# Four opening products taken in turns, norm factors folded into the operand operations, and two weight sums reordered in a two-layer encoder kernel

## The chip, the cores and the metric

The kernel runs on one core of one Trainium2 chip. The core has a matrix engine (TensorE, PE in the profile, with its weight loads as PEld), VectorE (DVE), ScalarE (ACT), GpSimd (POOL) and SyncE (SP). SP, ACT and POOL issue DMAs; a DMA that adds to its destination is issued from POOL here. The metric is the device time of one execution in microseconds, as the median of several runs; lower is better.

## What is computed

An encoder of two layers over 512 tokens and 16 learned ones (528 columns), width 1024. A layer is a feed-forward half step, a mixer of two parallel branches, and a second feed-forward half step; a norm closes the whole.

```python
def rmsnorm(x, g):
    return x * lax.rsqrt(jnp.mean(x * x, axis=-1, keepdims=True) + EPS) * g

def swiglu(x, w_gate, w_up, w_down):
    return (jax.nn.silu(x @ w_gate) * (x @ w_up)) @ w_down

for l in range(DEPTH):                                     # DEPTH = 2
    h = h + 0.5 * swiglu(rmsnorm(h, norm_gains[l, 0]), ffn_w_gate[l, 0], ...)
    h = h + mixer(rmsnorm(h, norm_gains[l, 1]), ...)       # GLA branch + attention branch, gated
    h = h + 0.5 * swiglu(rmsnorm(h, norm_gains[l, 2]), ffn_w_gate[l, 1], ...)
return rmsnorm(h, final_norm)[:, N_META:]
```

The hidden width of the feed-forward part, D_FF, is 2816. All data are float32.

## The kernel before

The hidden state stands in SBUF as eight chunks of 128 channels by 528 tokens. Every float32 product is made of three matmuls on rounded parts: each operand is split into `hi`, a copy rounded to the matrix engine's format, and `lo`, the rest; hi·hi, hi·lo and lo·hi are summed. The split of a weight of 128 x 1024 is one cast on ScalarE (`whi`, line 226) and one subtraction on VectorE (`wlo`, line 227). There are four buffers for `whi` and four for `wlo`, so the fifth weight's cast waits until the first weight's matmuls are done.

**The gate and up products.** The 2816 hidden columns are 11 pairs of 256. For each pair the product with x is a 2 x 2 block product (two hidden blocks, two token halves, the channels as even and odd chunks) carried out with seven block products instead of eight. `product_of_pair` makes one of them: four operand pairs (k = 0 to 3, chunks 2k and 2k+1), gate and up, three matmuls each, 24 matmuls of 128 x 264. Products 1, 2 and 4 use a weight block straight from memory (w11, w12, w22). The other four use weight sums: product 7 uses s3 = w21 - w11, product 6 uses s2 = w22 + s3, product 5 uses s1 = w21 + w22, product 3 uses s4 = s2 - w12.

`Weights.sums` makes these sums. ScalarE writes the negative of w11 or w12 (line 177); POOL then adds blocks with accumulating DMAs (line 182): s3 += w21, s2 += s3, s1 = w21 += w22, s4 += s2, one after the other in POOL's own order, each 512 KB. s2 and s1 are first loaded by SP into two short-lived buffers (`wsb`); the next pair's loads into these wait until the split of the old one, and for s2 also the add into s4, is done. `s3` and `s4` stand in three longer-lived buffers (`wsa`).

**The operands.** `Norm.pair` (line 432) makes one operand pair from two chunks: it scales both by the norm's gain (line 436), forms the four sums and differences `t12` and `t34` (lines 451 to 455), and splits seven blocks of 264 columns into `hi` and `lo` tiles `xc` (lines 443, 444, 448, 449). The factor of the root mean square (`rs`) comes later: eight squares (line 426) on ScalarE, seven adds (line 430) on VectorE, then the mean by a matmul with constants (line 398), a logarithm, an exponential and a Newton step.

**The order.** `ffn_steps` writes the order of the products out by hand. At the start of each of the four feed-forward parts, here called an opening, it is products 1 and 2 of pair 0, products 1 and 2 of pair 1, then products 6, 5, 7, 4 and 3 of pair 0, then product 6 of pair 1 and so on. Products 1, 6, 7 and 4 of a pair add into the same accumulator, and between them ScalarE copies it (`snapshot`, line 521): product 7 can begin only after the copy behind product 6, and product 4 only after the copy behind product 7. `use` keeps four weights split ahead (`AHEAD_MADE`) and six loads ahead (`AHEAD_FETCHED`).

The engines' own orders are not those of the code: a scheduler places each instruction in its engine's queue by its own estimate of when the operands are there, and the queue then runs in that order, each instruction waiting for what it needs. In the order before, the opening at the kernel's start runs 18 matmuls of product 1 of pair 0, 18 of product 2, 13 of product 1 of pair 1, and then comes back to the fourth operand pair. Two matmuls of product 6 of pair 1 and the means (line 398) stand ahead of product 4 of pair 0.

At the start of the kernel the loads stand on SP in this order: chunks 0 and 1, w11 in two halves, chunks 2-3, 4-5, 6-7, then w22, w12 and w21 of pair 0, w11 and w12 of pair 1 (lines 1018 to 1031, with line 172).

## Time and profile before

| | us |
|---|---|
| median of three runs | 2251.74 |
| the three runs | 2250.69, 2251.74, 2256.43 |
| the profiled execution | 2250.44 |
| its span, first to last instruction | 2248.3 |
| idle time of TensorE in the span | 45.3 |

The page gives busy time, share of the span and number of instructions of each engine. A row of waits reads: the waiting engine, tile and line, what it waited for, total us, times, longest us. A row of a timeline reads: start, duration, engine, line, operation, tiles, count, and in brackets the idle time ahead of it and what ended it. Matmuls are pipelined, so one lasts longer than the distance from one start to the next. Matmul records can be missing here and there.

### The profile page before, as it was taken

What the parts mean: (1) busy time and instruction counts of PE and PEld (TensorE: products, weight loads), DVE (VectorE), ACT (ScalarE), POOL (GpSimd) and SP (SyncE); (2) the same over time, 40 slices, a digit from 0 to 9 for tenths busy, and PEclk for the clock granted to TensorE, in tenths of its full rate; (3) what the DMA queues carried; (4) which work ended last, traced back from release to release, by engine and by line L of the source; (5) the groups of instructions that cost most, each with busy time, mean ns of one, the idle gap of its engine ahead of it and who ended that gap; (6) DMA issues with size and microseconds to landing.
All of it is one profiled execution on the core that took longest, in us unless ns stands there. A gap on an engine that the chain in (4) does not pass through costs nothing.

```text
span 2248.3 us, 39712 instructions
## 1 busy us (share of the span) xinstructions
PE 2203.0 (98%) x16482; PEld 2095.4 (93%) x16482; DVE 1516.9 (67%) x2399; ACT 1193.9 (53%) x1763; POOL 159.2 (7%) x186
## 2 busy tenths in 40 slices
PE   6999999999999999999999999999999999999997
PEld 6999999989999999999999999999788888989896
DVE  6656567486886676565696575675878767756566
ACT  7635354344785564453575363553557836536353
POOL 1111010000000010101011110100000001101010
PEclk9999999999999999999999999999999999999998
DMA  9858562211113485766667685622121136859561
GB/s 260 213 151 224 150 169 94 85 53 67 48 39 113 118 209 156 190 182 176 172 175 196 158 223 141 173 100 76 57 75 48 48 122 168 226 147 225 153 178 57
DMA packets 88612, 315.57 MB, mean 140 GB/s; under 512 B 9840, under 2 KB 12272, under 8 KB 88432
## 3 DMA queue, kind: packets, MB, share of 16 engines
q1 hardware_dynamic: 61136, 218.26, 28.0%
q0 software_dynamic: 25344, 92.29, 22.9%
q8 instruction: 129, 2.11, 0.4%
q10 hardware_dynamic: 1952, 2.50, 0.3%
q14 instruction: 51, 0.42, 0.1%
HBM read 264.77 MB, written 2.10 MB: 119 GB/s over the span
## 4 chain that ended last, share of the span: by engine, by line
PE 87%; DVE 5%; ACT 4%; DMA 3%; issue 1%; POOL 0%; DVEq 0%; SPq 0%; ACTq 0%; POOLq 0%
PE ss L515 37%; PE ss L392 27%; PE mm L392 13%; PE sm L392 2%; DMA w<-win 2%; PE sm L890 1%; DVE wlo L227 1%; PE ss L865 1%; ACT whi L226 1%; PE sm L906 1%; ACT t L375 1%; PE ss L398 1%; PE sm L907 1%; PE ss L866 1%; PE sm L715 0%
## 5 line engine op out<-in xcount | busy, mean ns | idle before, releaser
L515 PE MATMUL ss<-xc,whi 128*128 128x264 f32 (+1 forms) x4928 | 904.2, 285 | 20.6 <-ACT whi L226 14.1
L515 PEld LDWEIGHTS ss<-xc,whi 128*128 128x128 f32 x4928 | 766.9, 189 | 25.2 <-ACT whi L226 14.6
L515 PE MATMUL ss<-xc,wlo 128*128 128x264 f32 (+1 forms) x2464 | 701.6, 285 | 3.0 <-DVE wlo L227 3.0
L392 PE MATMUL ss<-g,whi 128*128 128x264 f32 (+2 forms) x2668 | 493.9, 301 | 0.0
L515 PEld LDWEIGHTS ss<-xc,wlo 128*128 128x128 f32 x2464 | 465.8, 189 | 5.2 <-DVE wlo L227 4.9
L392 PEld LDWEIGHTS ss<-g,whi 128*128 128x128 f32 x2668 | 388.4, 188 | 17.2
L392 PE MATMUL mm<-x,whi 128*128 128x264 f32 (+1 forms) x1712 | 385.9, 315 | 0.0
L226 ACT CAST whi<-w 128x1024 fp32r<-128x1024 f32 (+1 forms) x221 | 231.1, 1047 | 263.6 <-PE ss L392 119.9
L226 ACT CAST whi<-raw 128x1024 fp32r<-128x1024 f32 x190 | 199.3, 1049 | 298.6 <-PE mm L392 102.3
L227 DVE TENSOR_TENSOR wlo<-w,whi 128x1024 fp32r<-128x1024 f32 (+1 forms) x221 | 267.7, 1218 | 107.9 <-ACT whi L226 106.1
L392 PE MATMUL ss<-g,wlo 128*128 128x264 f32 (+2 forms) x1334 | 310.0, 301 | 0.0
L227 DVE TENSOR_TENSOR wlo<-raw,whi 128x1024 fp32r<-128x1024 f32 x190 | 232.0, 1221 | 102.1 <-ACT whi L226 98.9
L392 PEld LDWEIGHTS mm<-x,whi 128*128 128x128 f32 x1712 | 278.4, 188 | 17.0 <-issue 1.0
L392 PE MATMUL mm<-x,wlo 128*128 128x264 f32 (+1 forms) x856 | 266.1, 315 | 0.0
L392 PEld LDWEIGHTS ss<-g,wlo 128*128 128x128 f32 x1334 | 213.4, 188 | 8.7
L226 ACT CAST whi<-s 128x1024 fp32r<-128x1024 f32 x88 | 92.4, 1050 | 150.7 <-PE ss L515 131.1
L227 DVE TENSOR_TENSOR wlo<-s,whi 128x1024 fp32r<-128x1024 f32 x88 | 107.6, 1222 | 96.1 <-ACT whi L226 96.0
L392 PEld LDWEIGHTS mm<-x,wlo 128*128 128x128 f32 x856 | 159.6, 188 | 8.8 <-issue 1.0
L482 DVE SCALAR_TENSOR_TENSOR t<-ss,rs 128x528 f32<-128x528 f32 (+1 forms) x95 | 65.8, 699 | 127.9 <-PE ss L392 127.7
L177 ACT ACTIVATE s<-w 128x1024 f32<-128x1024 f32 x88 | 93.3, 1060 | 72.1 <-DMA w<-win 37.9
L182 POOL DMA_DIRECT2D w<-win x44 | 39.1, 889 | 954.5 <-DVE g L381 393.5
L521 ACT COPY snap<-ss 128x528 f32<-128x528 f32 (+1 forms) x132 | 77.1, 584 | 1.3 <-PE ss L515 1.3
(237 smaller groups left out, 2566.8 us busy)
## 6 DMA issues: line engine op xcount, KB each, us to landing
w<-win SPq DMA_DIRECT2D x219, 512.0 KB, 4.7
raw<-wts SPq DMA_DIRECT2D x190, 512.0 KB, 3.3
s<-win POOLq DMA_DIRECT2D x44, 512.0 KB, 7.7
w<-s POOLq DMA_DIRECT2D x44, 512.0 KB, 5.4
w<-win POOLq DMA_DIRECT2D x44, 512.0 KB, 7.0
s<-w POOLq DMA_DIRECT2D x44, 512.0 KB, 7.7
h<-xt SPq DMA_DIRECT2D x3, 528.0 KB, 6.8
out<-h SPq DMA_DIRECT2D x4, 256.0 KB, 2.3
```

The lines of the kernel that those rows point to most:

```text
L177: self.nc.scalar.activation(t, w, AF.Copy, scale=-1.0)
L182: self.nc.gpsimd.dma_start(t, src, accum_op=ALU.add)
L226: nc.scalar.copy(hi[:, cs], w[:, cs])
L227: nc.vector.tensor_tensor(lo[:, cs], w[:, cs], hi[:, cs].bitcast(F32), ALU.subtract)
L375: prev_act[0] = S.activation(*args, **kw).ins
L392: TE.matmul(acc.half[i][:width], lhs, rhs[:, acc.spans[i]], start=first, stop=last)
L398: TE.matmul(a, weights, x[:, hs], start=True, stop=True)
L482: V.scalar_tensor_tensor(cut(dst[rows]), pv[rows], -0.5 * f, cut(rs[rows]), ALU.mult, ALU.mult)
L515: TE.matmul(acc[:, j], a[:, j, k], b[:, at], start=bool(begin and k == 0 and i == 0), stop=k == len(x) - 1 and i == 2, skip_group_check=no ...
L521: S.copy(st[name], acc)
L865: TE.matmul(s[:n, i, :HF], lhs, kh[:, hs], start=True, stop=False)
L866: TE.matmul(s[:n, i, :HF], lhs, kl[:, hs], start=False, stop=True)
```

## The change

Three things are changed.

1. At the head of each feed-forward part the four products are one step, `opening`. It prepares all four weights and then runs the matmuls by operand pair: pair k = 0 and then k = 1 for products 1 and 2 of pair 0; k = 0 and 1 for product 1 of pair 1; the same for its product 2; then k = 2 for all four and k = 3 for all four. The copies and sums behind the products follow, and the weights beyond the fourth are split only there. `product_of_pair` is cut into `begin_product`, `multiply` and `finish_product`. Where the squares are made inside the feed-forward part, they are issued after the copy behind product 1 of pair 0.
2. `Norm.pair` no longer scales both chunks first: the gain goes into each cast, subtraction and difference as a factor, with a negated copy of the gains (`npt`) for the one block that is needed negative.
3. For pair 0 of the very first feed-forward part, s1 (w21 loaded, w22 added) is loaded and added right after s3, ahead of the add that makes s2. On SP the load of w12 now stands ahead of chunks 4-5, those of w22 and w21 ahead of chunks 6-7, and pair 1's w11 and w12 behind.

```diff
 def ffn_steps():
...
-        steps += [("P", p, c) for p in range(pair, pair + 1 + ahead) for c in "12"]
+        steps += [("O", tuple((p, c) for p in range(2) for c in "12"))] if ahead else [("P", pair, c) for c in "12"]
...
     def sums(self, f, i, product, w):
         got = self.summed
+        ahead = f + (i,) == (0, 0, 0)
         if product == "1":
             s3 = self.negative(f, i, "s3", w)
             self.add(s3, self.dram(f, i, "21"))
             s2 = self.block(f, i, "22", self.short, "wsb")
-            self.add(s2, s3)
             got[f, i, "7"], got[f, i, "6"] = s3, s2
+            if ahead:
+                got[f, i, "5"] = self.block(f, i, "21", self.short, "wsb")
+                self.before = self.add(got[f, i, "5"], self.dram(f, i, "22"))
+            else:
+                self.add(s2, s3)
         else:
-            s1 = self.block(f, i, "21", self.short, "wsb")
-            self.add(s1, self.dram(f, i, "22"))
+            if ahead:
+                with self.tc.issue_after(self.before):
+                    self.add(got[f, i, "6"], got[f, i, "7"])
+            else:
+                got[f, i, "5"] = self.block(f, i, "21", self.short, "wsb")
+                self.add(got[f, i, "5"], self.dram(f, i, "22"))
             s4 = self.negative(f, i, "s4", w)
             self.add(s4, got[f, i, "6"])
-            got[f, i, "5"], got[f, i, "3"] = s1, s4
+            got[f, i, "3"] = s4
...
-    def use(self, j):
-        self.make(j + AHEAD_MADE)
+    def use(self, j, ahead=AHEAD_MADE):
+        self.make(j + ahead)
         self.fetch(j + AHEAD_FETCHED)
...
+    V.tensor_scalar(npt, pt[:, :G_GN], -1.0, None, ALU.mult)
...
         def pair(self, j):
-            raw = [slot("t"), slot("t")]
-            for i, t in enumerate(raw):
-                S.activation(t, h(2 * j + i), AF.Identity, scale=col(self.gc + 2 * j + i))
             w = live[0] // 2
-            b11, b12, b21, b22 = [t[:, i : i + w] for t in raw for i in (0, w)]
+            b11, b12, b21, b22 = [h(2 * j + i, slice(a, a + w)) for i in (0, 1) for a in (0, w)]
+            g1, g2, minus = col(self.gc + 2 * j), col(self.gc + 2 * j + 1), npt[...]
...
+            V.tensor_tensor(t34[:, :w], b12, b11, ALU.subtract)
+            for at, b, g in ((0, b11, g1), (1, b21, g2), (6, b22, minus)):
+                S.activation(hi[:, at], b, AF.Identity, scale=g)
+                if at == 0:
+                    S.activation(t12[:, :w], t34[:, :w], AF.Identity, scale=g)
+                V.scalar_tensor_tensor(lo[:, at], b, g, hi[:, at].bitcast(F32), ALU.mult, ALU.subtract)
+            V.scalar_tensor_tensor(t12[:, w:], b22, g2, t12[:, :w], ALU.mult, ALU.subtract)
+            V.scalar_tensor_tensor(t34[:, :w], b11, g1, t12[:, w:], ALU.mult, ALU.subtract)
+            V.scalar_tensor_tensor(t34[:, w:], b21, g2, t12[:, w:], ALU.mult, ALU.subtract)
+            for at, t in ((slice(2, 4), v2(t12)), (slice(4, 6), v2(t34))):
+                S.copy(hi[:, at], t)
+                V.tensor_tensor(lo[:, at], t, hi[:, at].bitcast(F32), ALU.subtract)
...
+        def opening(some):
+            begun = [(c,) + begin_product(p, c, ahead=len(some) - i) for i, (p, c) in enumerate(some)]
+            for which, ks in ((begun[:2], (0,)), (begun[:2], (1,)), (begun[2:3], (0, 1)), (begun[3:], (0, 1)),
+                              (begun, (2,)), (begun, (3,))):
+                for t in which:
+                    multiply(*t, ks)
+            for i, ((p, c), t) in enumerate(zip(some, begun)):
+                finish_product(p, c, t[1])
+                if i:
+                    W.make(W.at[(l, f), 0, "2"] + 3 + i)
...
                 if step[1:] == (0, "5") and norm.acc is None:
-                    for c in range(KC):
-                        norm.square(c)
+                    with after(made[0]["opened"]):
+                        for c in range(KC):
+                            norm.square(c)
...
     for c in (2, 4, 6):
         nc.sync.dma_start(hall[:, c : c + 2], xt[:, c : c + 2])
-    W.make(1)
-    W.fetch(2)
+        if c == 2:
+            W.fetch(2)
+        elif c == 4:
+            W.make(1)
+    W.fetch(3)
     first.pair(1)
     W.make(2)
-    W.fetch(3)
+    W.fetch(4)
     first.pair(2)
-    W.make(3)
-    W.fetch(4)
+    W.make(4)
     first.pair(3)
```

In the engines' orders that the scheduler makes of it, POOL's adds of pair 0 stand as s3, s1, s2, s4 (before: s3, s2, s1, s4). On ScalarE the copy behind product 7 of pair 0 stands after the cast of pair 1's s2 and before that of its s1 (before: after both). The means stand directly ahead of product 4 of pair 0, and no matmul of product 6 of pair 1 stands ahead of it in the first opening.

More of the change, by code (lines that the diff above doesn't have):

```diff
@@ L85, in ffn @@
                 plan.append(("op", (l, f)) + step[1:])
+            elif step[0] == "O":
+                plan.extend(("op", (l, f)) + t for t in step[1])
             else:
@@ L147, with __init__ @@
 class Weights:
-    def __init__(self, nc, raw, hi, lo, wts, win):
-        self.nc, self.raw, self.hi_pool, self.lo_pool, self.wts, self.win = nc, raw, hi, lo, wts, win
+    def __init__(self, tc, raw, hi, lo, wts, win):
+        nc = tc.nc
+        self.tc, self.nc, self.raw, self.hi_pool, self.lo_pool, self.wts, self.win = tc, nc, raw, hi, lo, wts, win
         self.long = self.short = None
@@ L180, in add @@
     def add(self, t, src):
-        self.nc.gpsimd.dma_start(t, src, accum_op=ALU.add)
+        return self.nc.gpsimd.dma_start(t, src, accum_op=ALU.add).ins
     def sums(self, f, i, product, w):
         got = self.summed
+        ahead = f + (i,) == (0, 0, 0)
         if product == "1":
@@ L255, in row, with op @@
         return [t[:, c : c + n * width] for t in self.got[self.at[s]]]
-    def op(self, *load):
+    def op(self, *load, ahead=AHEAD_MADE):
         assert PLAN[self.pos][1:] == load, (PLAN[self.pos], load)
         self.pos += 1
-        return [t.rearrange("p (w k m) -> p w k m", w=2, k=KC // 2) for t in self.use(self.at[load])]
+        return [t.rearrange("p (w k m) -> p w k m", w=2, k=KC // 2) for t in self.use(self.at[load], ahead)]
 def build(tc, ctx, xt, wts, win, par, w2, const, umask, out):
@@ L276, in build @@
     small = pool("small", 4)
-    W = Weights(nc, pool("wraw", 3), pool("whi", 4), pool("wlo", 4), wts, win)
+    W = Weights(tc, pool("wraw", 3), pool("whi", 4), pool("wlo", 4), wts, win)
     pss = pool("pss", 2, bass.MemoryType.PSUM)
@@ L321, in build @@
     pt = one.tile([P, NPAR], F32, name="par")
+    npt = one.tile([P, G_GN], F32, name="npar")
     ct = one.tile([P, NCONST], F32, name="const")
@@ L432, in pair @@
         def pair(self, j):
-            raw = [slot("t"), slot("t")]
-            for i, t in enumerate(raw):
-                S.activation(t, h(2 * j + i), AF.Identity, scale=col(self.gc + 2 * j + i))
             w = live[0] // 2
-            b11, b12, b21, b22 = [t[:, i : i + w] for t in raw for i in (0, w)]
+            b11, b12, b21, b22 = [h(2 * j + i, slice(a, a + w)) for i in (0, 1) for a in (0, w)]
+            g1, g2, minus = col(self.gc + 2 * j), col(self.gc + 2 * j + 1), npt[:, self.gc + 2 * j + 1 : self.gc + 2 * j + 2]
@@ L439, in pair @@
             hi, lo = [slots["xc"].tile([P, 7 * T // 2], F32R, tag="xc", name=nm("xc"))[:, : 7 * w]
                       .rearrange("p (s c) -> p s c", s=7) for _ in range(2)]
-            def parts(at, src):
-                S.copy(hi[:, at], src)
-                V.tensor_tensor(lo[:, at], src, hi[:, at].bitcast(F32), ALU.subtract)
-            parts(0, b11)
-            parts(1, b21)
-            S.activation(hi[:, 6], b22, AF.Copy, scale=-1.0)
-            V.scalar_tensor_tensor(lo[:, 6], b22, -1.0, hi[:, 6].bitcast(F32), ALU.mult, ALU.subtract)
@@ L450, in pair @@
-            t12, t34 = slot("t"), slot("t")
-            V.tensor_tensor(t12[:, :w], b12, b11, ALU.subtract)
-            V.tensor_tensor(t12[:, w:], b22, t12[:, :w], ALU.subtract)
-            parts(slice(2, 4), v2(t12))
-            V.tensor_tensor(t34[:, :w], b12, b22, ALU.subtract)
-            V.tensor_tensor(t34[:, w:], b21, t12[:, w:], ALU.subtract)
-            parts(slice(4, 6), v2(t34))
+            t12, t34 = slot("t"), slot("t")
+            V.tensor_tensor(t34[:, :w], b12, b11, ALU.subtract)
@@ L500, in ffn, with begin_product @@
         made, hid, sums = {}, {}, {}
-        def product_of_pair(p, product):
+        def begin_product(p, product, **ahead):
             kind = "s2" if p % 2 == 0 else "ss"
@@ L508, in product_of_pair, with multiply @@
                 st[where] = pair(kind == "s2")
-            acc = st[where][:, :, :w]
-            hi, lo = W.op((l, f), p, product)
+            return st[where][:, :, :w], W.op((l, f), p, product, **ahead), begin
+        def multiply(product, acc, parts, begin, ks):
+            hi, lo = parts
             at = PLACE[product]
-            for k, (xh, xl) in enumerate(x):
+            for k in ks:
+                xh, xl = x[k]
                 for j in range(2):
@@ L516, in product_of_pair, with finish_product @@
                                   stop=k == len(x) - 1 and i == 2, skip_group_check=not begin)
+        def product_of_pair(p, product):
+            acc, parts, begin = begin_product(p, product)
+            multiply(product, acc, parts, begin, range(len(x)))
+            finish_product(p, product, acc)
+        def opening(some):
[8 more added lines that the diff above has]
+                    W.make(W.at[(l, f), 0, "2"] + 3 + i)
+        def finish_product(p, product, acc):
+            st = made[p]
             def snapshot(name):
@@ L520, in snapshot @@
                 st[name] = v2(t)
-                S.copy(st[name], acc)
+                return S.copy(st[name], acc).ins
             if product == "1":
-                snapshot("p1")
+                st["opened"] = snapshot("p1")
             elif product == "2":
@@ L575, in ffn @@
         for i, step in enumerate(steps):
-            if step[0] == "P":
+            if step[0] == "O":
+                opening(step[1])
+            elif step[0] == "P":
                 if step[1:] == (0, "5") and norm.acc is None:
-                    for c in range(KC):
-                        norm.square(c)
+                    with after(made[0]["opened"]):
+                        for c in range(KC):
+                            norm.square(c)
                 product_of_pair(*step[1:])
```

## The prediction

> **What bounds the kernel now.** I read the page's head first, then what TensorE waited for, then its stretches, and last the queue of adds behind the longest wait.

> ```profile
> span 2248.3 us, 39712 instructions
> ...
> PE 2203.0 (98%) x16482; PEld 2095.4 (93%) x16482; DVE 1516.9 (67%) x2399; ACT 1193.9 (53%) x1763; POOL 159.2 (7%) x186
> PE ss L515 <- ACT whi L226: 14.1, 3, 7.9
> ```

> TensorE is busy 2203.0 of 2248.3 us, so whatever this change does is bounded by 45 us of idle time, plus stretches at a lower clock. The waits on a weight's cast (whi, L226) are three: 7.9 before the first matmul, one of 6.0, and the 0.2 left of the 14.1. The rows of that last one, TensorE and then ScalarE:

> ```profile
> 38.44 0.28 PE L515 MATMUL ss<-xc,wlo 128*128 128x264 f32 x1
> 44.72 0.81 PE L515 MATMUL ss<-xc,whi 128*128 128x264 f32 x2 [6.00 <-ACT whi L226]
> 45.33 1.96 PE L398 MATMUL ss<-t,const 128*128 128x264 f32 x4
> 47.78 0.81 PE L515 MATMUL ss<-xc,whi 128*128 128x264 f32 x2 [0.49 <-ACT snap L521]
> 43.62 1.04 ACT L226 CAST whi<-w 128x1024 fp32r<-128x1024 f32 x1 [4.00 <-DMA w<-s]
> 46.19 1.04 ACT L226 CAST whi<-w 128x1024 fp32r<-128x1024 f32 x1 [1.52 <-DMA w<-win]
> 47.14 0.59 ACT L521 COPY snap<-ss 128x528 f32<-128x528 f32 x1
> ```

> By the instruction order, 38.44 is the end of product 7 of pair 0. The two matmuls at 44.72 belong to product 6 of pair 1, whose weight sum had just landed; the four of L398 are the norm's means; product 4 of pair 0 begins only at 47.78. Its own weights were long there. It waited for the copy of the accumulator after product 7, and that copy stood on ScalarE behind two casts, the second of which waited for another sum. What this costs in clock:

> ```profile
> 22.00:25.40 3.40, 3.40 (x31) 3.40 (x30) 3.20 (x9) 3.40 (x8) 0.38 (x1) 1.00 1.01 177
> 38.70:44.70 6.00, 0.02 (x1) 0.00 (x0) 2.96 (x4) 1.97 (x2) 1.36 (x2) 0.82 1.06 240
> 44.70:52.70 8.00, 7.49 (x28) 6.54 (x29) 4.48 (x5) 4.38 (x6) 1.26 (x2) 0.50 0.71 163
> ```

> (Columns: stretch, length, busy time of PE, PEld, DVE, ACT, POOL, granted clock, DMA share, GB/s.) Full clock runs 31 matmuls in 3.4 us, 0.12 us each when nothing waits. After the empty stretch the granted clock is 0.50 until 52.70: of the 4.92 us from 47.78 to 52.70, half, some 2.4 us, is clock.

> Behind the two late sums stands one queue, POOL's accumulating DMAs, in order:

> ```profile
> 9.67 1.02 POOL L182 DMA_DIRECT2D s<-win  x1 [9.22 <-ACT s L177]
> 19.75 0.87 POOL L182 DMA_DIRECT2D w<-s  x1 [9.06 <-DMA s<-win]
> 20.30 1.23 POOL L182 DMA_DIRECT2D w<-win  x1
> 25.02 0.88 POOL L182 DMA_DIRECT2D s<-w  x1 [3.50 <-ACT whi L226]
> 37.82 0.85 POOL L182 DMA_DIRECT2D w<-s  x1 [11.02 <-DVE t L430]
> 9.67 9.78 DMA s<-win
> 20.30 9.15 DMA w<-win
> 39.05 7.06 DMA w<-win
> s<-w POOLq DMA_DIRECT2D x1, 512.0 KB, 7.9
> w<-s POOLq DMA_DIRECT2D x1, 512.0 KB, 5.7
> ```

> The three rows naming DMA are from the chain of waits (start, duration), the last two from the DMA issues of a short stretch each (the one at 25.02 and the one at 37.82; last column, issue to landing). So pair 0's sums land at 19.45 (s3), 29.45 (s1), 32.9 (s4); pair 1's s2 at 37.82 + 5.7 = 43.5, its s1 at 46.11. The row at 37.82 names DVE L430, which has nothing to do with it; its load, issued when s4 had landed and freed the buffer, is what arrives then.

> **The change, part by part. 1. Pair 0's s1 add ahead on POOL, loads regrouped.** The new order on POOL is s3, s1, s2, s4 of pair 0; on SP, w12 before the last two operand chunks, w21 and w22 between them, and pair 1's two weights last. How the transfers share the engines:

> ```profile
> q1 hardware_dynamic: 664, 2.46, 103.2%
> q0 software_dynamic: 127, 0.48, 61.5%
> q1 hardware_dynamic: 158, 0.58, 39.6%
> q0 software_dynamic: 209, 0.77, 102.7%
> ```

> The first row is from 7.5 to 13.5 (loads alone: 410 KB/us, 1.3 us for 512 KB), the next two are one stretch of 4.0 us, 14.3 to 18.3 (both: 145 KB/us for loads, 120 for adds), the last is 29.6 to 33.4 (adds alone: 203 KB/us, 2.6 us). The bytes before s4 lands are the same; nothing becomes cheaper, only the order changes. s3 starts as before, since ScalarE's negation comes after the same work: at best 0.3 us sooner, at worst 0.3 later. While it and s1 stream, loads crawl: a 512 KB load takes 3.6 us. The last operand chunks, just begun at 14.3, have their rest by about 17.3, pair 1's w11 is there at 20.9 and its w12 at 24.5. Then cast and subtraction,

> ```profile
> L226 ACT CAST whi<-w 128x1024 fp32r<-128x1024 f32 (+1 forms) x221 | 231.1, 1047 | 263.6 <-PE ss L392 119.9
> L227 DVE TENSOR_TENSOR wlo<-w,whi 128x1024 fp32r<-128x1024 f32 (+1 forms) x221 | 267.7, 1218 | 107.9 <-ACT whi L226 106.1
> ```

> 1.05 + 1.22, and about 35 matmuls of the four products that need this weight or stand behind it, 4.3 us, make 31.1; a landing is later than the last byte, and I take T = 32 for the start of product 6 of pair 0. Before it was about 29.3: 24 x 3 matmuls, 8.8 us, and some 0.4 of waits ahead of 38.44. So this part alone costs 2.7 us of TensorE's early lead; on the path that sets the end it costs nothing as long as the sums are later still, and product 7 ends at T + 8.9 = 40.9.

> s2 and s4 of pair 0 come behind s1 and so later by up to 2.6 us, but s4 loses the competitor it had (it took 7.9): I put it at 32.5 (31.5 to 34). Pair 1's w22 load then, and its s2 at 42.5, against 43.5; bounds 41.5 and 44.5.

> **2. Four products in turns, and what ScalarE does between.** In the new order ScalarE casts pair 1's s2 weight, then copies the accumulator, and only then casts s1's. So product 4 no longer waits for the sum that lands at 46.11: 42.5 + 1.05 + 0.59 = 44.1, and no matmul of product 6 of pair 1 stands ahead of it. The means stand ahead of it instead. Their squares now start after the copy of product 1:

> ```profile
> L426 ACT ACTIVATE t<-h x8: 637/642/651, 32.9 to 38.1; 128x528 f32<-128x528 f32 x8
> L430 DVE TENSOR_TENSOR t<-t,t x7: 700/708/711, 34.9 to 41.1; 128x528 f32<-128x528 f32 x7
> ```

> Before, first square to last add took 32.9 to 41.8, 8.9 us, with one 1.22 us subtraction in between that now comes after. The four casts and two copies ahead of them take 4.9 us from the end of product 1 at T - 1.9: squares at 35.0, sums at 42.7, means done 0.9 later at full clock (1.96 at half, row at 45.33) = 43.6. The two ways agree; product 4 starts at about 44.3 instead of 47.78: **-3.4 us**. Bounds: 43.4 if sums and loads run as fast as their best rows, 47.0 if T slips by 3.

> **3. The clock.** TensorE's empty stretch shrinks from 6.0 us to less than 2 (40.9 to 42.7) and a short one behind the means. I take the clock as kept: **-2.4 us**; the other end is 0, if it falls all the same. [...]

> **4. Given back.** The two matmuls done early before (0.24) and a wait for the bank of pair 0's first accumulator, since the rsqrt still waits behind the sum of 46.1 on ScalarE: **+0.5** (0 to 1.5).

> **5. The other three openings.** Their idle time, waits of the stretches 780 to 830, 1140 to 1175 and 1880 to 1920:

> ```profile
> PE ss L515 <- ACT snap L521: 1.2, 1, 1.2
> PE ss L515 <- ACT xc L443: 0.5, 1, 0.5
> PE ss L398 <- DVE t L430: 0.5, 1, 0.5
> PE ss L515 <- ACT snap L521: 1.6, 1, 1.6
> ```

> The 1.2 and 1.6 are again the copy behind a cast that waits for a sum; the copy now precedes that cast, which leaves some 0.3. Against it, taking turns frees the first weight buffer only 18 matmuls (2.2 us) before product 6 needs it, while cast and subtraction take 2.3: 0.2 to 0.5 lost, and the copy after product 6 now stands behind the means' logarithm: 0.3. The third opening loses its 0.5 on xc, since the operand comes straight from h. Together **-1.6** (bounds -3.5 and +1.5).

> **6. Norm factors inside the operations.** Per operand pair ScalarE loses two 528-wide scalings and gets one of 264:

> ```profile
> L436 ACT ACTIVATE t<-h,par x8: 718/726/735, 4.0 to 21.7; 128x528 f32<-128x528 f32 x8
> 6.39 0.42 ACT L448 ACTIVATE xc<-t 128x264 fp32r<-128x264 f32 x1
> ```

> 2 x 0.73 - 0.42 = 1.0 us less per pair; VectorE keeps its nine operations per pair, and one negation of 48 columns comes at the start (well below 0.42). Both engines work beside a busy TensorE (67% and 53%), and the opening waits for weights and sums: 0. Without that cover it would be 4 us per opening.

> Sum: -3.4 - 2.4 + 0.5 - 1.6 = -6.9 against the profiled execution's 2250.44 us (span 2248.3): 2243.5. The median of the runs shown is 2251.74, 1.3 above it, the lowest 2250.69; I add half a microsecond for that: **2244.2 us**.

> **Rivals.** *A: the clock stays low through the opening.* The first matmuls run at half pace, in the timeline:

> ```profile
> 15.61 0.64 PE L515 MATMUL ss<-xc,whi 128*128 128x264 f32 x2
> 24.28 0.40 PE L515 MATMUL ss<-xc,whi 128*128 128x264 f32 x2
> ```

> Two take 0.64 against 0.40, so one starts 0.22 after the other against 0.12. In the new order some 38 matmuls are done by 19, and the next need pair 1's first weight, cast at 22: whether the clock rises before that gap of 3 us and survives it is open. If not, the 35 matmuls cost up to 4.3 more, part of it until the clock rises: T slips by 2 to 3, product 4 starts at 46.7, and the sum is -1.0 - 2.4 + 0.5 - 1.6: 2246.5. [...] *B: the sums are hidden behind nothing new.* All bytes still go through the same engines; if pair 1's s2 lands at 44.5 and T at 34, the clock falls again: only -1.7 + 0.5 - 1.0, 2248.7. For it: the DMA share is about 1.0 up to 34 us. Against: the copy no longer waits for s1. *C: slower.* The adds, now in a row, starve pair 1's loads: if loads get nothing from 14.3 while s3, s1 and s2 stream (7.8 us), and s4 takes 2.6 of the time that three loads then need (3.9), w12 lands at 28.6; cast, subtraction and 35 matmuls at double the 0.12 (8.5) give T = 39.4, and product 4, 12.3 later as in the forecast, 51.7: +3.9, no clock gained, +0.5 - 1.6: 2253.7. It decides from T = 36. The row of 145 KB/us for loads beside adds speaks against it. *D: the change doesn't do what it says* (the scheduler took turns already: it ran 18, 18 and 13 matmuls of three products before it came back with the fourth operand); then only the copies' place matters, 43.62 + 1.05 + 0.59 = 45.3 instead of 47.78: 2247.3, near B.

> **Chances.** Forecast 0.57 (2240.5 to 2246.0 for itself), A 0.20, B and D 0.12, C 0.06, better than 2240.5 0.05. A measurement of this kernel tells about 0.3%, 6.8 us, from no change: faster means under 2245.0. Seven tenths of the forecast, a third of A and all of the last: 0.52 faster; slower is most of C and a little for other mishaps, 0.06; the rest, 0.42, within. The range 2239.5 to 2250.0 takes in A and B and leaves out C.

> **What would show it.** The four openings' matmuls end near 32 and the idle wait of 6.0 is gone; product 4 starts by 45 with the copy ahead of the cast on s1's weight; the granted clock stays 1.00 from 40 to 56; s1 of pair 0 lands near 24, pair 1's s2 near 42.5; the copies' waits at the later openings fall to 0.3. Wrong would be: a clock of 0.50 between 20 and 36, a T over 34, or a new wait for a cast ahead of product 6 at the later openings.

## The result and the profile after

| | before | after |
|---|---|---|
| median of 20 runs each, us | 2251.46 | 2256.65 |
| lowest to highest | 2249.28 to 2256.43 | 2254.38 to 2260.87 |
| the profiled execution | 2250.44 | 2258.68 |

The ratio is 1.0023, 95% interval 1.0016 to 1.0029: 5.2 us slower, where 7 us faster was forecast. The two profiled executions stand 8.2 apart; that of after is 2.0 above its median.

The head of the page of after, and what TensorE waited for (total us, times, longest):

```profile
span 2256.9 us, 39694 instructions
...
PE 2207.2 (98%) x16482; PEld 2101.8 (93%) x16482; DVE 1522.9 (67%) x2400; ACT 1186.0 (53%) x1747; POOL 159.2 (7%) x186
```

```profile
PE ss L529 <- ACT whi L239: 17.6, 5, 7.6
PE ss L529 <- DVE wlo L240: 5.6, 8, 1.3
...
PE ss L529 <- ACT snap L555: 3.0, 1, 3.0
```

The 6.0 us wait of before is gone from the first row, yet its sum has grown from 14.1 to 17.6: two new waits of 3.9 have come, both at later openings. To see where the time went, I take the start of every matmul in the profiled execution (16482 records in each trace), minus the start of the one with the same number in before, and then how much this difference grows over each opening:

| us, against the profile of before | 1st | between | 2nd | 3rd | between | 4th | span |
|---|---|---|---|---|---|---|---|
| after | -1.85 | +1.16 | +5.59 | +0.02 | -0.64 | +4.20 | +8.60 |

(The openings are taken as 0 to 60, 780 to 835, 1140 to 1200 and 1880 to 1925 us of before; a few hundredths between the second and third, and the tail, are left out of the table.) So the loss is at the second and fourth opening. The chain at the second opening, first ScalarE, SP and POOL before, then the same in after with TensorE, each with the issue row of that add (last column, issue to landing):

```profile
795.25 1.05 ACT L226 CAST whi<-w 128x1024 fp32r<-128x1024 f32 x1 [0.88 <-PE ss L515]
797.58 0.33 SPq L172 DMA_DIRECT2D w<-win  x1
801.48 0.86 POOL L182 DMA_DIRECT2D w<-s  x1 [18.41 <-DMA w<-win]
w<-s POOLq DMA_DIRECT2D x1, 512.0 KB, 6.0
```

```profile
799.55 1.05 ACT L239 CAST whi<-w 128x1024 fp32r<-128x1024 f32 x1 [3.90 <-PE ss L529]
801.88 0.33 SPq L176 DMA_DIRECT2D w<-win  x1
806.02 0.86 POOL L186 DMA_DIRECT2D w<-s  x1 [25.85 <-DVE wlo L240]
w<-s POOLq DMA_DIRECT2D x1, 512.0 KB, 8.4
814.47 1.04 ACT L239 CAST whi<-w 128x1024 fp32r<-128x1024 f32 x1 [4.85 <-DMA w<-s]
815.42 1.05 ACT L181 ACTIVATE s<-w 128x1024 f32<-128x1024 f32 x1
816.38 0.57 ACT L555 COPY snap<-ss 128x528 f32<-128x528 f32 x1
815.57 0.81 PE L529 MATMUL ss<-xc,whi 128*128 128x264 f32 x2 [3.91 <-ACT whi L239]
816.83 0.59 PE L529 MATMUL ss<-xc,wlo 128*128 128x264 f32 x1 [0.45 <-DVE wlo L240]
```

The first cast in both is that of pair 0's s2, the weight of product 6. In after it waits 3.90 us for TensorE, because with turns the first split buffer is held until the end of the opening. Only when that cast and its subtraction are done is the buffer of s2 free, so the load of pair 1's s2 is issued 4.3 us later (801.88 against 797.58), its add 4.5 later, and the add then takes 8.4 us instead of 6.0: it lands at 814.4 instead of 807.5, after the time it is wanted. Two loads start 0.5 and 1.1 us behind this add; in before they start 1.5 and 3.7 behind it. TensorE does not go on with product 4, for two reasons: in its own order six matmuls of product 6 of pair 1 stand ahead of product 4 here (13 in before), and the copy that product 4 needs stands on ScalarE behind the late cast, too. The granted clock is 0.50 from 814.8 to 821.6. The fourth opening repeats it (wait of 3.93 at 1916.51).

In the first opening the copy ahead of product 4, in after (ScalarE, TensorE, and the issue row of the add behind the cast):

```profile
44.44 1.04 ACT L239 CAST whi<-w 128x1024 fp32r<-128x1024 f32 x1 [3.82 <-DMA w<-s]
45.40 0.59 ACT L555 COPY snap<-ss 128x528 f32<-128x528 f32 x1
41.93 1.13 PE L413 MATMUL ss<-t,const 128*128 128x264 f32 x4 [1.71 <-issue]
46.04 0.81 PE L529 MATMUL ss<-xc,whi 128*128 128x264 f32 x2 [2.98 <-ACT snap L555]
w<-s POOLq DMA_DIRECT2D x1, 512.0 KB, 5.5
```

Product 4 starts at 46.04, 1.7 us earlier than before, not 3.4; the copy still waits for pair 1's s2. The granted clock is 0.50 from 43.4 to 50.2, and also from 22.9 to 26.3, where it was 1.00 in before.

### The profile page after: what moved, and what is told of

It is laid out like the page before. It is cut to its first block, busy times and chain, and to the rows that moved or that the text cites. A ratio compares the mean times of both kernels' runs of the same rounds, so it can differ in the third digit from the quotient of the medians.

```text
span 2256.9 us, 39694 instructions
## 1 busy us (share of the span) xinstructions
PE 2207.2 (98%) x16482; PEld 2101.8 (93%) x16482; DVE 1522.9 (67%) x2400; ACT 1186.0 (53%) x1747; POOL 159.2 (7%) x186
## 4 chain that ended last, share of the span: by engine, by line
PE 89%; DVE 4%; ACT 3%; DMA 2%; issue 1%; SPq 0%; DVEq 0%; ACTq 0%; POOLq 0%
PE ss L529 38%; PE ss L407 28%; PE mm L407 14%; PE sm L407 2%; DMA w<-s 1%; PE sm L927 1%; DMA w<-win 1%; DVE wlo L240 1%; PE ss L902 1%; ACT whi L239 1%; PE sm L943 1%; PE sm L944 1%; PE ss L903 1%; PE ss L413 1%; PE sm L752 0%
## 5 line engine op out<-in xcount | busy, mean ns | idle before, releaser
L529 PE MATMUL ss<-xc,whi 128*128 128x264 f32 (+1 forms) x4928 | 908.3, 286 | 20.6 <-ACT whi L239 17.6
L239 ACT CAST whi<-w 128x1024 fp32r<-128x1024 f32 (+1 forms) x221 | 231.1, 1046 | 274.5 <-PE ss L407 118.6
## 6 DMA issues: line engine op xcount, KB each, us to landing
w<-win SPq DMA_DIRECT2D x219, 512.0 KB, 4.7
raw<-wts SPq DMA_DIRECT2D x190, 512.0 KB, 3.4
s<-win POOLq DMA_DIRECT2D x44, 512.0 KB, 6.8
w<-win POOLq DMA_DIRECT2D x44, 512.0 KB, 7.1
w<-s POOLq DMA_DIRECT2D x44, 512.0 KB, 5.4
s<-w POOLq DMA_DIRECT2D x44, 512.0 KB, 7.5
```

The lines of the kernel that those rows point to most:

```text
L239: nc.scalar.copy(hi[:, cs], w[:, cs])
L529: TE.matmul(acc[:, j], a[:, j, k], b[:, at], start=bool(begin and k == 0 and i == 0), stop=k == len(x) - 1 and i == 2, skip_group_check=no ...
```

## The experiments

The theory: what matters in each opening is when the accumulating DMA of pair 1's s2 lands; turns make it later because the s2 buffer is freed later. Rival F: the folding or the regrouped loads do it. Rival G: chance of the clock. All ratios are against the kernel before, with their 95% intervals; after all runs stands one table of the openings.

**Turns in the first opening only**, the rest of the change kept:

```diff
-def ffn_steps():
+def ffn_steps(turns=True):
...
+        if ahead and turns:
+            steps += [("O", tuple((p, c) for p in range(2) for c in "12"))]
+        else:
+            steps += [("P", p, c) for p in range(pair, pair + 1 + ahead) for c in "12"]
...
+        for step in ffn_steps((l, f) == (0, 0)):
```

> The four products are taken in turns in the first opening only; the other three openings run product after product, with the norm factors folded and the sums ahead as in the changed kernel. Theory (turns hold all four split buffers to the end of an opening, so product 6's sum is cast some 4 us later, its buffer comes free later and pair 1's load and add behind it land too late): the 3.9 us waits on the cast ahead of product 6 of pair 1 at the second and fourth opening are gone (below 1 us, as before), pair 1's s2 lands there as early as before, the first opening keeps its gain of about 1.8 us: 2249.7 us, 0.999 of the kernel before (2248 to 2251.5). Rival F (the folded norm factors or the regrouped loads shift the later openings): the waits of 3.9 us stay, 2256 us. Rival G (the loss is only where the half-clock window happens to fall): the waits stay about as they are and the time lies anywhere from 2250 to 2257.

Measured: 2254.29 us, ratio 1.0013 (1.0004 to 1.0023). At the second and fourth opening +0.09 and +0.46: the waits on the cast there are gone, as the theory says, and against F and G for these two. The time is above its range all the same, for the third opening, which had lost nothing in after, loses 4.8. The theory did not foresee that:

```profile
1170.55 0.81 PE L532 MATMUL ss<-xc,whi 128*128 128x264 f32 x2 [2.62 <-ACT whi L242]
```

**Turns in the later openings only** (the condition reversed):

> The opposite: turns in the second to fourth opening only, product after product in the first; folding and sums ahead kept. Theory: both 3.9 us waits ahead of product 6 of pair 1 and the half clock behind them stay, about +5 at the second opening and +4 at the fourth against the kernel before, the first opening without its gain or with part of it: 2257.5 us (2255 to 2260). Rival F: no different from the changed kernel in the later openings either, so this run alone does not tell F from the theory; with turns_first it does. Rival G: 2250 to 2257 without the two waits tied to the same place.

Measured: 2260.05 us, 1.0036 (1.0024 to 1.0049), at the upper end of its range. The second and fourth opening lose +3.4 and +3.0, with waits of 2.45 and 2.56 instead of 3.9: the place as expected, the size smaller. The first opening without turns is 2.1 slower than before instead of faster.

**No turns**, folding and sums ahead kept (condition `False`):

> No turns anywhere: folding and the sums and loads ahead remain. Theory: later openings as before (no wait over 1 us ahead of product 6 of pair 1), first opening within 2 us of before: 2250.5 us (2248 to 2253). Rival F: 2255 or more, with the waits of 3.9 us at the second and fourth opening.

Measured: 2259.95 us, 1.0036 (1.0024 to 1.0049): a miss. The second and fourth opening are clean (-0.19, +0.27), but the first costs +3.7 and the third +4.8. So something beside the turns costs time. What costs it in the first opening was not followed up; the third is taken up under folding.

**Turns alone**, without folding and with sums and loads as before:

> Turns in all four openings, but the norm scales its chunks first and the sums and loads stand as before. Theory: the two waits of about 3.9 us and the loss of some 4 to 5 us each at the second and fourth opening are there without the other two parts; the first opening within 2 us of before: 2257.5 us (2255 to 2261). Rival F: no such waits, 2251.5 us.

Measured: 2266.01 us, 1.0061 (1.0047 to 1.0074), above its range. The two losses are there without the other parts (+5.1 and +4.9), with waits of 2.88 and 4.28 on the cast. The third opening, which the forecast left out, loses 5.7 here as well, in other waits (1.8 for the sum of squares, 2.4 for a copy).

**Folding alone** (the kernel before with `Norm.pair` and `npt` of after):

> The kernel before with the norm factors folded into the operand operations, and nothing else. The run without turns lost 4.8 us at the third opening, and so did the one with turns in the first opening only; turns without folding lost 5.3 there. Theory: an operand that is ready earlier, or buffers that come free earlier, let loads start beside the accumulating DMA of pair 1's s2, which then lands later than its use; so folding by itself costs 4 to 5 us at the third opening, nothing over 0.6 us at the second and fourth, and 0 to 2 us in the first (another order there): 2257 us (2255 to 2260). Rival: folding is free, as forecast, and the third opening's loss belongs to the regrouped sums or to a chance of the clock: 2252 us (2250.5 to 2254).

Measured: 2255.68 us, 1.0014 (1.0005 to 1.0022). Folding is not free: +4.8 at the third opening, nothing at the second and fourth. The third opening in before and in this run, ScalarE's negation, POOL's add of pair 1's s2, SP's two next loads (one row for both in the second trace) and the add's issue row:

```profile
1161.56 1.06 ACT L177 ACTIVATE s<-w 128x1024 f32<-128x1024 f32 x1
1161.34 0.86 POOL L182 DMA_DIRECT2D w<-s  x1 [25.91 <-DVE wlo L227]
1162.64 0.33 SPq L172 DMA_DIRECT2D w<-win  x1
1163.47 0.77 SPq L172 DMA_DIRECT2D w<-win  x1
w<-s POOLq DMA_DIRECT2D x1, 512.0 KB, 5.4
```

```profile
1163.22 1.07 ACT L177 ACTIVATE s<-w 128x1024 f32<-128x1024 f32 x1
1164.06 0.86 POOL L182 DMA_DIRECT2D w<-s  x1 [25.94 <-DVE c L526]
1164.32 0.80 SPq L172 DMA_DIRECT2D w<-win  x2
w<-s POOLq DMA_DIRECT2D x1, 512.0 KB, 8.9
```

The negation frees the buffer into which the first of these loads goes. In before it ends 1.3 us after the add is issued; with a lighter norm ScalarE gets to it earlier, and it ends 0.2 after. The two loads then start beside the add, which takes 8.9 us instead of 5.4. In the run with turns in the first opening only the same add, with the first load 0.5 us behind it, takes 8.5; in after, with 2.3, it takes 6.6. Whether the loads are the cause, the next run tests. One more thing changes in this run at this opening. On ScalarE the copy behind product 7 stood ahead of the cast of pair 1's s1, and now stands after it (before, then this run):

```profile
1171.52 0.59 ACT L521 COPY snap<-ss 128x528 f32<-128x528 f32 x1
1172.70 1.06 ACT L226 CAST whi<-w 128x1024 fp32r<-128x1024 f32 x1
```

```profile
1176.00 1.05 ACT L226 CAST whi<-w 128x1024 fp32r<-128x1024 f32 x1 [0.98 <-DMA w<-win]
1176.95 0.59 ACT L519 COPY snap<-ss 128x528 f32<-128x528 f32 x1
```

**Loads held behind the add** (turns in the first opening only, and at the third opening SP must wait for the sum):

```diff
                 self.add(s2, s3)
+                if f + (i,) == (1, 0, 1):
+                    self.hold = self.nc.sync.dma_start(self.scratch, s2[:, :8]).ins
...
+        if self.hold is not None and pool is None and f + (i, name) in ((1, 0, 2, "12"), (1, 0, 1, "22")):
...
+            with self.tc.issue_after(hold):
+                w = self.block(f, i, name, pool, tag)
```

> The kernel with turns in the first opening only, and at the third opening SP's next two loads (pair 2's w12 and pair 1's w22 for product 4) held behind the landing of pair 1's s2 add, by a transfer of 8 columns of that sum that SP's queue has to wait for. Without the hold they were issued 0.5 and 0.9 us after the add, which took 8.5 us (5.4 in the kernel before, where they came 1.3 and 2.1 after it). Theory L (loads that start right beside the add slow it): the add takes 5 to 6 us, TensorE's wait of 3.9 us at the third opening shrinks by 2 us or more, 2251 us (2249.5 to 2253). Rival M: the add takes over 8 us all the same, no change, 2254 us. Rival N: the add is fast, but the held loads are then late themselves and give the time back: 2253 to 2256 us, the wait stands on those weights.

(The 3.9 us in this expectation belongs to the first opening of that run; at the third its wait was the 2.62 shown above.) Measured: 2251.62 us, 0.9998 (0.9989 to 1.0007). The rows of the third opening (POOL, SP, the add's issue row, ScalarE, TensorE):

```profile
1163.98 0.86 POOL L195 DMA_DIRECT2D w<-s  x1 [25.80 <-ACT whi L250]
1168.83 0.53 SPq L213 DMA_DIRECT2D scratch<-w  x1
w<-s POOLq DMA_DIRECT2D x1, 512.0 KB, 4.8
1173.46 1.04 ACT L250 CAST whi<-w 128x1024 fp32r<-128x1024 f32 x1 [2.55 <-DMA w<-win]
1174.41 0.59 ACT L567 COPY snap<-ss 128x528 f32<-128x528 f32 x1
1175.05 0.39 PE L541 MATMUL ss<-xc,whi 128*128 128x264 f32 x1 [1.86 <-ACT snap L567]
```

The add takes 4.8 us, and the wait on the cast is gone: with every engine's order here the same but for the hold on SP, loads beside the add are what slowed it (M falls). A new wait of 1.86 behind a copy gives half of it back: the opening loses 2.55 instead of 4.77. It does not stand on the held weights, as N had it. The copy stands behind the cast of pair 1's s1, which starts when that sum lands, at 1173.46 here and at 1173.33 without the hold. So a second cost lies behind the first: the copy's new place, which the late s2 had hidden. The profiled execution is the slowest of this kernel's eleven, so the time rests on the median.

**A third s2 buffer, and its control.** Both have four instead of six buffers for `t`, which makes the room; only one has the third buffer. On TensorE, VectorE and ScalarE all instructions stand in the same order, on POOL those of the openings; on SP the loads of s2 and s1 move ahead, since they have a buffer earlier, so the expectation's "on every engine" is too wide by this one queue.

```diff
-    slots = {n: pool("s_" + n, b) for n, b in dict(g=16, t=6, rs=2).items()}
+    slots = {n: pool("s_" + n, b) for n, b in dict(g=16, t=4, rs=2).items()}
...
-        pools = open_pools("left", wsa=3, wsb=2)
+        pools = open_pools("left", wsa=3, wsb=3)
```

> Control for the next run: the changed kernel with four instead of six buffers for the norm's short-lived tiles (t), which makes room in SBUF. The orders of the second and fourth opening are those of the changed kernel, so both waits of 3.9 us ahead of product 6 of pair 1 stay: 2257 us (2255 to 2261).

> The control with a third buffer for the short-lived weight sums (s1, s2); the instructions stand in the same order on every engine. Theory: at the second and fourth opening the load of pair 1's w22 no longer waits for the split of pair 0's s2, it is issued several us earlier, its add lands before about 810 and 1912 us, both 3.9 us waits and the half clock behind them go: 4 to 5 us less at each, some 8 to 10 us less than the control (2247 to 2249 us). Rival R1: the wait stems from the engines' order in turns (the copy behind the cast) or from the adds' bandwidth, not from the buffer: within 2 us of the control, the waits over 3 us. The first opening is bound by transfers in both theories: no more than 2 us from the control there.

Measured: control 2259.85 us, 1.0034 (1.0021 to 1.0046); with the buffer 2249.43 us, 0.9988 (0.9979 to 0.9997), 10.4 less (R1 falls). The control has the two waits as expected by place, but they are 2.15 and 3.07 us instead of 3.9. The second opening, the add of pair 1's s2 and TensorE's longest wait in product 6 of pair 1, control first:

```profile
808.44 0.86 POOL L186 DMA_DIRECT2D w<-s  x1 [25.45 <-DVE wlo L240]
816.38 0.51 PE L529 MATMUL ss<-xc,whi 128*128 128x264 f32 x2 [2.15 <-ACT whi L239]
```

```profile
791.81 0.86 POOL L186 DMA_DIRECT2D w<-s  x1 [8.59 <-DMA s<-win]
814.88 0.39 PE L529 MATMUL ss<-xc,wlo 128*128 128x264 f32 x1 [0.64 <-DVE wlo L240]
```

The add is issued 16.6 us earlier, and the waits on the cast disappear while the orders of the computing engines stay: the buffer is what the turns were short of. In the first opening four `t` buffers put two matmuls of product 6 of pair 1 ahead of product 4 again, which fits its loss of 1.3 where after gains 1.9. There the two kernels agree (+1.33 and +1.21): TensorE goes on with product 6 of pair 1 at 47.70 and 47.45, after waits of 5.90 and 7.49 for the cast of its s2. That is within the 2 us of the expectation; that transfers are the limit there was not shown.

**Pair 0 finished first** (its two products over all four operand pairs, then those of pair 1, still as one step):

```diff
-            for which, ks in ((begun[:2], (0,)), (begun[:2], (1,)), (begun[2:3], (0, 1)), (begun[3:], (0, 1)),
-                              (begun, (2,)), (begun, (3,))):
+            for which, ks in ((begun[:2], (0,)), (begun[:2], (1,)), (begun[:2], (2,)), (begun[:2], (3,)),
+                              (begun[2:3], (0, 1, 2, 3)), (begun[3:], (0, 1, 2, 3))):
```

> The opening as one step, all four weights ready first, but the two products of pair 0 are finished over all four operand pairs before those of pair 1 are taken, so the first two split buffers come free about 5 us earlier than in turns. Folding and sums ahead stay. Theory: no wait over 1.2 us ahead of product 6 of pair 1 at the second and fourth opening, each within 0.6 us of the kernel before; the first opening, where the engines' order is that without turns, loses 2 to 4 us, the third gives 0 to 5: 2256 us (2253.5 to 2260). Rival R2 (it is having all four weights split first, not the turns): the 3.9 us waits stay.

Measured: 2259.79 us, 1.0031 (1.0021 to 1.0042). The casts' waits ahead of product 6 of pair 1 are 0.37 and 0.41 at the second and fourth opening, so R2 falls; each still loses 1.1, more than the 0.6 expected, and why was not followed up. First (+2.2) and third opening (+5.1) lose as they do without turns. At the third the copy stands ahead of the cast of s1 here, and TensorE waits 2.04 us for the cast of pair 1's s2: the late sum is enough for a loss, without the copy's new place.

**Parts put together.** Turns in the first opening and the folding for the first norm only, with the first sums and loads ahead, all else as before; then the changed kernel with a third s2 buffer from the second part on (six `t` and two s2 buffers in the first part); then the same with turns in the first opening only.

```diff
         def pair(self, j):
+            if self.gc != G_NORM:
+                return self.scaled(j)
```

```diff
-        pools = open_pools("left", wsa=3, wsb=2)
+        pools = open_pools("left", wsa=3, **(dict(wsb=2, tx=2) if W.long is None else dict(wsb=3)))
```

(`scaled` is the method of before; every third `t` of the first part comes from `tx`.)

> Turns in the first opening only, the norm factors folded only for the first norm, the first sums and loads ahead: the first opening has the orders of the changed kernel, the other three those of the kernel before. Theory (each opening's gain or loss stands by itself): -1.9 us at the first opening and nothing at the others, up to +1.5 for a dip of the clock at about 580 us: 2250 us (2248 to 2252), no wait over 2 us at the later openings. If the parts act on each other across openings, 2253 or more.

> The changed kernel with a third buffer for s1 and s2 in the second to fourth opening, and in the first part two and six buffers (sums, t) as in the changed kernel, so that the first opening keeps its order. Theory: the first opening's -1.9 us as in the changed kernel, the second to fourth as in the run with three buffers (about -0.9, -1 and -1 us against the kernel before), up to +1.5 for the dip at 580: 2247 us (2245 to 2249.5). Rival (the first opening's gain costs the next what it gives): 2249.5 or more.

> The same buffers, turns in the first opening only. It tells what turns are worth at the later openings once the buffer is there, and whether the third buffer also takes away the third opening's 4.8 us that folding costs without turns. Theory: the add of pair 1's s2 is issued earlier, so no wait over 2 us at any later opening; turns give under 2 us of their own there: 2248.5 us (2246.5 to 2251). Rival: the third opening's loss does not hang on when the add is issued: it stays, 2253 us.

Measured: 2250.79 us, 0.9996 (0.9987 to 1.0005); 2246.85 us, 0.9981 (0.9972 to 0.9990); 2246.97 us, 0.9977 (0.9968 to 0.9987). The last two beat both kernels. Between them there is no difference that can be told, so with the buffer there, turns at the later openings are worth nothing measurable. The buffer also helps where there are no turns: with turns in the first opening only, the second to fourth opening go from +0.09, +4.77 and +0.46 to -1.47, -0.28 and -1.87. With turns and four `t` buffers the second and fourth gain more from it, 4.1 and 5.9, as a chain that turns had made late should.

| us, profile against that of before | 1st | 2nd | 3rd | 4th | span |
|---|---|---|---|---|---|
| turns in the first opening only | -1.93 | +0.09 | +4.77 | +0.46 | +3.76 |
| turns in the later openings only | +2.10 | +3.40 | -0.49 | +3.04 | +7.76 |
| no turns | +3.69 | -0.19 | +4.82 | +0.27 | +9.60 |
| turns alone | -0.31 | +5.06 | +5.66 | +4.86 | +16.04 |
| folding alone | +1.43 | -0.03 | +4.78 | 0.00 | +6.52 |
| loads held | +0.52 | -0.51 | +2.55 | +1.61 | +5.35 |
| four t buffers (control) | +1.33 | +3.21 | +0.41 | +4.62 | +9.77 |
| third s2 buffer, four t | +1.21 | -0.92 | -0.93 | -1.25 | -0.65 |
| pair 0 first | +2.18 | +1.05 | +5.06 | +1.11 | +9.76 |
| first turns and first folding | -1.91 | -0.03 | +0.20 | +1.58 | +0.55 |
| third buffer later, turns | -2.54 | -0.91 | -0.95 | -1.24 | -3.36 |
| third buffer later, first turns | -2.78 | -1.47 | -0.28 | -1.87 | -3.97 |

One execution each, so a line can be some us off its median. What a row lacks to its span lies between the openings and in the tail, in most rows in the stretch near 580 us told of below (2.1 of it in the last two rows). "Loads held" has the first opening's orders of "turns in the first opening only", yet +0.52 against -1.93; its pair 1's s2 landed at 46.8 against 43.8. Its fourth opening, too, has +1.61 in orders that gave +0.46.

## Why the prediction was wrong, by its steps

- **Step 5, the other three openings, is the one that failed.** It said -1.6 with bounds -3.5 and +1.5; the profile has +9.8 (5.59 + 0.02 + 4.20). The step saw that turns free the first weight buffer late, and priced only the wait of the cast behind it, 0.2 to 0.5. It did not follow that cast to the next thing that hangs on it: the s2 buffer, the load into it, the add, and then the two things behind the cast of that sum, six matmuls in TensorE's own order and the copy on ScalarE. The run with the third buffer shows that this chain is the loss; the runs with turns in one place only show that it goes with the turns. The copy did move ahead of the cast of s1, as the step said, but now stands, with one negation between, behind the cast that became late. The last part of the prediction did name a new wait ahead of product 6 as what would refute it.
- **Step 6, folding at nothing, failed too**, though after does not show it: alone it costs 3.8 us between the medians. The cover named, a busy TensorE, was there. What I left out was what a lighter ScalarE sets free, a buffer and with it loads that collide with an add, and that ScalarE's order changes with it. Holding these loads brought the add from 8.5 to 4.8 us and took away about half of the loss; the copy that waits behind the cast of s1 accounts for the rest by the trace, but no run moved it alone. That after loses nothing at its third opening fits the loads 2.3 us behind its add; no run varied that distance alone with turns.
- **Step 1** was right for TensorE: product 6 of pair 0 starts at 31.0 (forecast 32), s4 lands at 33.1 (32.5). Pair 1's s2 landed at 44.4, at the edge of its bounds, not 42.5: load and add after s4 took 11.3 us, not 10. That a landing comes behind the last byte is in the trace of before: the last 4 KB packet of s3's add ends at 18.95, the add lands at 19.45. The bytes are the same, as the step itself says; rival B put this landing at 44.5 and was right in it, though the product's start at 34 that it went with did not come.
- **Step 2** has the mechanism right and the size off by that landing: product 4 at 46.0, not 44.3, -1.7 instead of -3.4 and inside its bounds.
- **Step 3, the clock kept, was wrong**: it fell at 43.4. The step counted one empty stretch of less than 2 us and only "a short one behind the means". That a wait this short keeps the clock, and with it the -2.4 us, was my assumption, and no run shows that term: after a wait of 1.61 us at the fourth opening of before the granted clock stayed at 1.00, after one of 1.67 with first turns and first folding it was 0.50. The two waits of 1.71 and 2.98 have only four matmuls between them, and 6.8 us at 0.50 followed instead of 10.2. The first opening's net, -1.85 us, stands against the -5.3 of steps 2 to 4. The clock was low between 22.9 and 26.3 as well, a sign of being wrong that the prediction names with rival A, but product 6 of pair 0 started no later for it than forecast.
- **Between the openings** a stretch of half clock near 580 us explains most of the +1.16. It has no wait of its own (below) and appears in eight of the runs too, in others not; one of the eight has no turns, another neither the folding nor the regrouped loads, so no one edit makes it.
- **A slip in the sum**: from 2243.5 to 2244.2 it adds 0.7, not the half microsecond that it names. Nothing hangs on it.

That the change does what it says (rival D) is shown by its orders. Not tried: the kernel before with a third s2 buffer, whose room would have to come from the `t` tiles of its unfolded norm. So how much of the 4.5 us that the last two kernels gain needs the change at all stays open.

## What to carry to other kernels

When a step holds a buffer longer, price not the instruction that waits for it but everything that instruction frees in turn: here a cast that waited 3.90 us, a sum buffer, its load 4.3 us later, an add of 8.4 us instead of 6.0, and the copy queued on ScalarE behind the cast of that sum. An edit that lightens an engine with time to spare need not be free either: here folding alone cost 3.8 us, with two loads started beside an awaited add, which took 8.9 us instead of 5.4. Ask which buffer a new order leans on: one more where the chain hung was worth 10 us with turns in every opening, and with it there turns at the later openings were worth nothing that could be told. When you take one delay away, look at what had been waiting in its shadow: with the loads held it was a wait of 1.86 us behind the copy.

## What the runs showed of the hardware

The granted clock fell here without an empty stretch ahead of it. Stretches of 3.4 us (PE, PEld, DVE, ACT, POOL busy, granted clock, DMA share, GB/s) of after's first opening and of the fourth opening with first turns and first folding:

```profile
40.00:43.40 3.40, 1.35 (x6) 0.69 (x5) 2.75 (x4) 0.63 (x1) 0.87 (x1) 1.00 1.08 229
43.40:46.80 3.40, 0.76 (x3) 0.76 (x4) 1.28 (x2) 1.54 (x2) 0.88 (x1) 0.50 0.91 167
```

```profile
1907.50:1910.90 3.40, 1.67 (x12) 1.47 (x12) 0.62 (x2) 1.53 (x2) 0.00 (x0) 1.00 1.07 223
1910.90:1914.30 3.40, 3.40 (x16) 3.40 (x17) 1.63 (x3) 0.00 (x0) 0.00 (x0) 0.50 0.95 196
```

```profile
575.90:579.30 3.40, 3.40 (x31) 3.38 (x30) 1.89 (x5) 1.99 (x6) 0.00 (x0) 1.00 0.00 0
579.30:582.70 3.40, 3.40 (x18) 3.33 (x17) 2.80 (x9) 2.02 (x5) 0.00 (x0) 0.50 0.00 0
```

Why stays open. And 512 KB of an accumulating DMA took 4.8 us with loads held and 8.5 with two loads issued 0.5 and 0.9 us behind it, in the same order of the computing engines.
